# An encoder layer on one NeuronCore: order of the vector work behind a head norm, order of the indexer's items, other PSUM banks for the sample's products, a later spill and a later residual scaling

## The chip, the core and the metric

The kernel runs on one NeuronCore of one Trainium2 chip, in one launch. The metric is the time on the device in microseconds, and lower is better. The kernel before takes 1190.45 us, the median of three runs (1190.23 to 1190.97).

## What is computed

One layer of a streaming encoder, in float32, for two groups of tokens that share all weights: 512 tokens of a prompt and 32 tokens of a sample. They are handled as one block of 544 columns, two halves of 272. The model width is 1024.

```python
x = post_norm(x, swiglu1(modulate(x, sh1, sc1)), 1 + gt1, 0.5)
h = modulate(x, sh2, sc2)
rq, rk, rv, rg, aq, ak, av, iq, ik, iw = split(h @ w_in)      # 33 blocks of 128 columns
ret = head_norm(retention(rq, rk, rv)) * silu(rg)             # 4 heads, chunkwise recurrence
score = sum_over_heads(iw * relu(iq @ ik.T))                  # the indexer, 8 heads
keys  = top_k(score, 128)                                     # admissible keys alone
att   = softmax(aq @ ak[keys].T) @ av[keys]                   # 8 heads; rotary on aq, ak, iq, ik
x = post_norm(x, concat(ret, att) @ w_out, 1 + gt2, 1.0)
x = post_norm(x, swiglu2(modulate(x, sh3, sc3)), 1 + gt3, 0.5)
```

`post_norm` is a layer norm of `ALPHA * x + weight * gate * out`. The sample also has 512 earlier keys and values and an earlier retention state, which are inputs. Outputs are the new x of both groups, their keys, values and indexer keys, and the retention states.

## The kernel before

**Products.** Each operand of a large product is split into a high and a low part (`float32r`); a product is three matmuls (`mm3`, line 140). A weight block of 128 columns is loaded raw (`wr_w`, on SP's queue), ScalarE rounds it (line 129, a CAST) and negates the rounded part (line 133), and a DMA on GpSimd's queue adds the raw block to that, which leaves the low part (line 134). For some blocks VectorE subtracts instead (line 136). A weight is split three products ahead of its use (`AHEAD`, `next_w`).

**Order of the work.** The order of TensorE's instructions is written by hand: each matmul is tied to the one before (`ordered("pe", ...)`, lines 66 to 78; the tie is an order of issue, not a wait). The raw loads are tied in the same way. The other engines' orders are made by the framework when the program is built: where an engine is free in its own model of the times, it takes among the instructions that are ready the one that was written first. On the chip each engine then runs its list in that fixed order, and an instruction whose input is late holds up all behind it. `tc.high_priority()` puts the instructions written inside it ahead of others that are ready; `add_manual_dep(..., NOSYNC)` only fixes that one comes behind another in such a list.

**Ticks.** Side work is written as Python generators (`jobs`, lines 81 to 98). The main line calls `tick()` after each half of a projection, which is 24 matmuls of 272 columns; a job that says `yield n` goes on n ticks later. So a tick is a place in the written order, about 3 to 5 us of TensorE's time in the middle stage.

**The middle stage** (the mixer), about 440 to 720 us. The main line projects `h` on 33 weight blocks: indexer first, then for each retention head hh its q, k and v (`retention`, line 853), then for each pair c of attention heads its k, q and v (`pair_inputs`, line 975), then four gates (line 1159). Beside it run these jobs:

- `indexer` (line 752): ten items. An item is 6 to 12 products of indexer queries `iq[c]` with the keys `iks`, for a token tile t of 128 rows and c's of two heads each; into two PSUM banks (one of tag `l`, one of tag `o`), which ScalarE's relu empties (line 767) and VectorE adds up into `work[t]` (lines 772, 774). Tile 1 takes two items, tiles 2 and 3 four each. Then the sample's two groups (`isg`, line 782) follow.
- `topk` (line 796), for tiles 1, 2, 3 and the sample: 16 or 17 steps of MAX8 (line 803) and MATCH_REPLACE8 (line 804) each on VectorE, two steps a tick for the tiles, one for the sample. It begins when tile 1 has its scores, and sets the flag `("mask", t)` when a tile is done.
- `side` of each retention head (line 879): its products, then `head_norm` (line 939), a chain of small VectorE operations on the products that ScalarE copied (line 917); two ticks later ScalarE applies it (line 925, five operations), and one tick later TensorE transposes the result (`rot`, line 929).
- `roped` of each pair (line 986): rows of k and q that take part in the rotary go by DMA to `rp`, VectorE turns them (`rope_turn`, lines 624 to 626), they go back, and `parts` (lines 646, 647) splits k and q.
- `attention` (line 1062): for each pair three groups n of tiles: `logits` (`lg`, two banks of tag `l`), a tick or two later the transposes of the weights (`pt`, two banks of tag `t`), then the products with the values.
- `sample_attention(g)` (line 1013), g = 0 and 1: waits for `("mask", 's')` and for a pair's attention; its logits go into two banks (`sl`, `sl2`), two ticks later transposes into two more (`spt`, `spt2`), which ScalarE copies (lines 1044, 1046).
- `spill` (line 816): x, in the four tiles `xr`, goes to DRAM to make room; `reload` (line 1131) brings it back, and scales it by the layer norm in eight steps, one a tick: two VectorE operations (line 1138) and one on ScalarE (line 1140). The output projection adds to it (line 270).

**PSUM** has eight banks: three of tag `a` (which the projections' halves use in turn), two of `l`, two of `t`, one of `o`. A product into a bank waits until the bank's last reader is done.

Of the kernel before, what the change touches and what calls it, by code (L numbers as in the profile page):

```python
# [16 lines left out]
P = 128  # L17
# [20 lines left out]
def encoder_layer_kernel(ctx, tc, xT, cT, wc1, w_e, w_cond, b_condT, lnp, w_gu1, w_dn1, w_in, w_out, w_gu2, w_dn2,  # L38
# [51 lines left out]
    def spawn(job):  # L90
        resume(job, now[0] + 1)
# [31 lines left out]
    def split_w(raw, n, name, lo_eng=None, pool=None, pin=False, src=None):  # L123
        if pool is None:
            hl = wh.tile([P, 2, ND, P], FR, name=f"wh_{name}", tag="wh")
            hi, lo = hl[:, 0], hl[:, 1]
        else:
            hi, lo = (pool.tile([P, ND, P], FR, name=f"wu_{name}", tag="u") for _ in range(2))
        c = nc.scalar.copy(hi[:, :n, :], raw[:, :n, :])  # L129
        if pin:  # L130
            tc.keep_in_program_order(c)
        if src is not None and lo_eng is None:
            nc.scalar.mul(lo[:, :n, :], hi[:, :n, :].bitcast(F32), -1.0)  # L133
            nc.gpsimd.dma_start(lo[:, :n, :], src, accum_op=ALU.add)  # L134
        else:
            r = (lo_eng or nc.gpsimd).tensor_tensor(lo[:, :n, :], raw[:, :n, :], hi[:, :n, :].bitcast(F32), op=ALU.subtract)
            last["lo"] = r.ins.name
        return hi, lo
# [482 lines left out]

    def rope_turn(rp, *zs):
        r = rp[0:32 * len(zs)]
        behind(nc.vector.stream_shuffle(r[:, 1, :], r[:, 0, :], SWAP), "evac")
        nc.vector.tensor_mul(r, r, tabA[0:32 * len(zs)])
        nc.vector.tensor_add(r[:, 0, :], r[:, 0, :], r[:, 1, :])
        for slot, z in enumerate(zs):
            nc.sync.dma_start(z[ROT], rp[32 * slot:32 * slot + 32, 0, :])
# [123 lines left out]
    def indexer():  # L752
        nc.vector.memset(work[0], 0.0)
        nc.vector.memset(work[0][0:64, 64:128], NEG)
        flags.add(("mask", 0))
        yield 0
        for t in range(1, 4):
            L = P * (t + 1)
            acc = work[t]
            n = 512 // L  # L760
            for c in range(0, 4, n):
                pair = [bank("l", "isc"), bank("o", "isc")]
                pair_products([[p[:, L * e:L * e + L] for e in range(n)] for p in pair],
                              [(iq[c + e], iks, t) for e in range(n)])
                for s in range(2):
                    rl = scr("rl")
                    nc.scalar.activation(rl[:, :n * L], pair[s][:, :n * L], AF.Relu)
                    for e in range(n):
                        hh = 2 * (c + e) + s
                        r, f = rl[:, L * e:L * e + L], iw[:, t, hh:hh + 1]  # L770
                        if hh == 0:
                            nc.vector.tensor_scalar(acc, r, f, None, op0=ALU.mult)
                        else:
                            nc.vector.scalar_tensor_tensor(acc, r, f, acc, op0=ALU.mult, op1=ALU.add)
                yield 1
            nc.vector.memset(acc[0:64, L - 64:L], NEG)
            flags.add(("score", t))
            if t == 1:
                spawn(topk())
        psA, psB = bank("a", "iss"), bank("o", "iss2")  # L780
        for g in range(2):
            ps, p2 = bank("l", "isg"), bank("l", "isg2")
            lq = iqz[:, 128 * g:128 * g + 128]
            mm(ps, lq, cik, start=True, stop=True)
            mm(p2[:, 0:32], lq, ikn, start=True, stop=True)
            rl = scr("rls")
            nc.vector.tensor_scalar(rl[:, 0:512], ps, 0.0, iws[:, g:g + 1], op0=ALU.max, op1=ALU.mult)
            nc.vector.tensor_scalar(rl[:, 512:544], p2[:, 0:32], 0.0, iws[:, g:g + 1], op0=ALU.max, op1=ALU.mult)
            yield 1
            mm(psA, sel, rl[:, 0:512], start=(g == 0), stop=(g == 1))  # L790
            mm(psB[:, 0:32], sel, rl[:, 512:544], start=(g == 0), stop=(g == 1))
        nc.scalar.copy(work['s'][:, 0:512], psA)
        nc.scalar.copy(work['s'][:, 512:544], psB[:, 0:32])
        flags.add(("score", 's'))

    def topk():
        for t, rate in ((1, 2), (2, 2), (3, 2), ('s', 1)):
            while ("score", t) not in flags:
                yield 1
            w = work[t]  # L800
            for n in range(17 if t == 's' else 16):
                m8 = sm.tile([P, 8], F32, name="m8", tag="m8")
                behind(nc.vector.max(m8, w), "pe")  # L803
                nc.vector.match_replace(w, in_to_replace=m8, in_values=w, imm_value=MARK)  # L804
                if n % rate == rate - 1:
                    yield 1
            nc.vector.tensor_scalar(w, w, -3.3e38, NEG, op0=ALU.is_gt, op1=ALU.mult)
            if t != 's':
                L = P * (t + 1)
                nc.vector.memset(w[0:64, L - 64:L], NEG)  # L810
            flags.add(("mask", t))
# [2 lines left out]
    project(taken(qs[3]))  # L814

    def spill():
        yield 0
        for j in range(4):
            nc.sync.dma_start(xd[j], xr[j].rearrange("p a t -> p (a t)"))

# [32 lines left out]
    def retention(hh):  # L853
# [25 lines left out]
        def side():  # L879
# [39 lines left out]
            nc.vector.scalar_tensor_tensor(so2, S0, GAM[hh] ** 32, ps2, op0=ALU.mult, op1=ALU.add)  # L919
            nc.sync.dma_start(st_s[hh], so2)  # L920
            normed = [(on[:, n * P:(n + 1) * P], P) for n in range(4)] + [(on2[0:32], 32)]
            w = head_norm(normed)
            yield 2
            for j, (x, rows) in enumerate(normed):
                nc.scalar.activation(x, x, AF.Identity, bias=w[:rows, 2, j:j + 1], scale=w[:rows, 1, j:j + 1])
# [13 lines left out]
    def head_norm(parts):  # L939
# [12 lines left out]
        for _ in range(3):  # L952
            nc.vector.scalar_tensor_tensor(z, y, -0.5, y, op0=ALU.mult, op1=ALU.mult)
            nc.vector.tensor_tensor(z, z, v, op=ALU.mult)
            nc.vector.scalar_tensor_tensor(y, z, 1.5, y, op0=ALU.add, op1=ALU.mult)
        nc.vector.scalar_tensor_tensor(w[:, 2], mv[:, :, 0], -1.0, w[:, 1], op0=ALU.mult, op1=ALU.mult)
        return w


# [53 lines left out]
    def sample_attention(g):  # L1013
# [5 lines left out]
        if g == 0:  # L1019
            yield 3  # L1020
        yield from wait_for(("mask", 's'), ("att", 2 * g + 1))
        ps, p2 = bank("l", "sl"), bank("l", "sl2")
        for j in range(4):
            c = 2 * g + j // 2
            lq = Vs[c][:, 1, 32 * (j % 2):32 * (j % 2) + 32]
# [10 lines left out]
        nc.vector.tensor_max(m, mx[:, 0:1], mx[:, 1:2])  # L1036
        softmax_rows(Pt, m)
        yield 2
        pt, pt2 = bank("t", "spt"), bank("t", "spt2")
        for t in range(4):  # L1040
            turned(pt[:, t * P:(t + 1) * P], Pt[:, t * P:(t + 1) * P], ident)
        turned(pt2[0:32, 0:P], Pt[:, 512:544], ident)
        PT = pu[:, 1, 0:512]
        nc.scalar.copy(PT, pt)
        PT2 = half_scr("PsT2", [P, P])
        nc.scalar.copy(PT2[0:32], pt2[0:32, 0:P])
        yield 1
        po = bank("l", "spo")
        pcs = [po[own(j % 2), 32 * (j // 2):32 * (j // 2) + 32] for j in range(4)]
# [81 lines left out]
    def reload():  # L1131
        for j in range(4):
            load(xr[j].rearrange("p a t -> p (a t)"), xd[j])
        yield 3
        for d in range(ND):
            x = xv(xr, d)
            for i, (a, b) in enumerate(HALVES):
                behind(nc.vector.scalar_tensor_tensor(x[:, a:b], x[:, a:b], al1[0][:, d:d + 1], rs1[i], op0=ALU.mult,
                                                      op1=ALU.mult), "pe")
            nc.scalar.activation(x, x, AF.Identity, bias=al1[1][:, d:d + 1])  # L1140
            yield 1
# [197 lines left out]
```

## Time and profile before

| | us |
|---|---|
| median of the runs | 1190.45 |
| the profiled execution: its own time | 1189.48 |
| its span, first to last instruction | 1187.4 |
| TensorE busy in it | 1159.3 |
| VectorE, ScalarE, GpSimd busy | 665.8, 586.7, 199.7 |

The profile is of one execution. "PE" is TensorE's matmuls, "PEld" its weight loads, "DVE" VectorE, "ACT" ScalarE, "POOL" GpSimd, "SP" the queue that issues most DMAs. L75 is line 75, the helper through which all matmuls go, L78 that of the transposes, so that groups are told apart by the names of tiles: `isc<-iks,iqs` is a product into the tile `isc`. In the timeline a row is: start, duration, engine, line, operation, output<-inputs, shape, how many; in brackets the idle time before it and what ended that. In the windows' table each row is one stretch of time, with the busy time of each engine, the clock that TensorE was granted (1.00 is full), the busy share of the DMA engines and GB/s.

### The profile page before, as it was taken

To read this page: it belongs to the slowest core of one execution; us is meant where nothing else is said; L and a number is where in the kernel's file an instruction comes from. 1 tells how busy PE (TensorE), PEld (TensorE's weight loads), DVE (VectorE), ACT (ScalarE), POOL (GpSimd) and SP (SyncE) were. 2 spreads that over 40 slices of the span, in tenths; PEclk is the share of its full clock that TensorE was granted. 3 is DMA by queue.
4 is the path that set the end of the run, shared out by engine and by line. 5 is a ranking of instruction groups with operands and counts; after the bars stand their busy time and mean duration, and the time that the engine had idled before them with its cause. 6 is when DMAs were issued, how large, how long until landed. Compare 5 with 4: busy or idle time off the path is not lost.

```text
span 1187.4 us, 23002 instructions
## 1 busy us (share of the span) xinstructions
PE 1159.3 (98%) x9419; PEld 1127.8 (95%) x9419; DVE 665.8 (56%) x1574; ACT 586.7 (49%) x990; POOL 199.7 (17%) x231
## 2 busy tenths in 40 slices
PE   9999999999999999899989999999999999999995
PEld 7999999999999999789979989999999999999995
DVE  5767665764468484677887775885542222201416
ACT  3644444444335364655466577546444444433423
POOL 0112111111111303312111101104111111111110
PEclk9999999999999999999989999999999999999998
DMA  9899999997999466644845588807988878788842
GB/s 359 293 297 308 239 256 229 258 215 183 296 259 215 119 222 168 149 116 115 193 100 162 132 257 225 209 31 197 263 177 175 177 175 173 163 173 176 177 88 76
DMA packets 71451, 231.41 MB, mean 195 GB/s; under 512 B 8657, under 2 KB 12881, under 8 KB 71345
## 3 DMA queue, kind: packets, MB, share of 16 engines
q0 software_dynamic: 23472, 83.37, 40.3%
q1 hardware_dynamic: 47728, 146.43, 35.5%
q8 instruction: 74, 1.21, 0.4%
q14 instruction: 33, 0.26, 0.1%
q10 hardware_dynamic: 144, 0.14, 0.0%
HBM read 220.54 MB, written 7.35 MB: 192 GB/s over the span
## 4 chain that ended last, share of the span: by engine, by line
PE 89%; DVE 4%; DMA 4%; ACT 2%; issue 1%; SPq 0%; DVEq 0%; ACTq 0%
PE gu L75 40%; PE dn L75 26%; PE in L75 15%; DMA we_raw<-in_w_e 3%; PE gu_e L75 2%; PE po L75 1%; PE pt L78 1%; DMA wh_w<-in_w_gu 1%; PE ro L75 1%; PE lg L75 1%; PE isc L75 1%; ACT wh_w L129 0%; DMA cm<-in_cmat 0%; DVE wk L804 0%; ACT wh_w L133 0%
## 5 line engine op out<-in xcount | busy, mean ns | idle before, releaser
L75 PE MATMUL gu<-h,wh_w 128*128 128x272 f32 x3840 | 482.7, 288 | 0.6 <-DMA wh_w<-in_w_gu 0.6
L75 PEld LDWEIGHTS gu<-h,wh_w 128*128 128x128 f32 x3840 | 481.4, 188 | 0.8 <-DMA wh_w<-in_w_gu 0.8
L75 PE MATMUL dn<-hid,wh_w 128*128 128x272 f32 x2112 | 266.6, 288 | 0.0
L75 PEld LDWEIGHTS dn<-hid,wh_w 128*128 128x128 f32 x2112 | 265.4, 188 | 0.2
L129 ACT CAST wh_w<-wr_w 128x1024 fp32r<-128x1024 f32 (+1 forms) x162 | 165.6, 1024 | 152.9 <-PE dn L75 102.1
L75 PE MATMUL in<-h,wh_w 128*128 128x272 f32 x1392 | 189.9, 294 | 0.0
L75 PEld LDWEIGHTS in<-h,wh_w 128*128 128x128 f32 x1392 | 179.6, 191 | 5.3 <-issue 3.4
L133 ACT ACTIVATE wh_w<-wh_w 128x1024 fp32r<-128x1024 f32 (+1 forms) x158 | 163.7, 1037 | 2.9
L556 DVE SCALAR_TENSOR_TENSOR ca<-wc,cz,ca 128x1024 f32<-128x1024 f32 x98 | 129.7, 1349 | 26.5 <-DMA wc<-in_w_cond 26.2
L134 POOL DMA_DIRECT2D wh_w<-in_w_gu x79 | 69.2, 876 | 408.8 <-ACT wh_w L133 333.6
L190 DVE TENSOR_TENSOR tnh<-tnh,gu 128x272 f32<-128x272 f32 x80 | 35.0, 437 | 123.1 <-PE gu L75 123.1
L188 ACT ACTIVATE tnh<-gu 128x272 f32<-128x272 f32 x80 | 31.8, 397 | 112.9 <-PE gu L75 112.7
L189 DVE SCALAR_TENSOR_TENSOR tnh<-tnh,gu 128x272 f32<-128x272 f32 x80 | 34.7, 435 | 84.3 <-ACT tnh L188 84.1
L191 ACT CAST hid<-tnh 128x272 fp32r<-128x272 f32 x88 | 36.7, 418 | 88.9 <-DVE tnh L190 88.9
L134 POOL DMA_DIRECT2D wh_w<-in_w_dn x48 | 41.7, 870 | 224.7 <-ACT wh_w L133 215.4
L270 DVE SCALAR_TENSOR_TENSOR xq<-dn,C,xq 128x272 f32<-128x272 f32 (+2 forms) x48 | 18.0, 404 | 105.2 <-PE dn L75 105.2
L192 DVE TENSOR_TENSOR hid<-tnh,hid 128x272 fp32r<-128x272 f32 x88 | 40.7, 464 | 39.2 <-ACT hid L191 38.2
L134 POOL DMA_DIRECT2D wh_w<-in_w_in x29 | 25.3, 885 | 136.2 <-ACT Pu L964 30.9
L803 DVE MAX8 m<-wk 128x8 f32<-128x544 f32 (+3 forms) x65 | 38.8, 598 | 0.7
L804 DVE MATCH_REPLACE8 wk<-m,wk 128x544 f32<-128x544 f32 (+3 forms) x65 | 38.0, 584 | 0.0
L75 PE MATMUL gu_e<-h,we 128*128 128x272 f32 x192 | 27.3, 296 | 0.5 <-ACT h L510 0.4
L75 PEld LDWEIGHTS gu_e<-h,we 128*128 128x128 f32 x192 | 24.8, 188 | 2.4 <-issue 1.0
(266 smaller groups left out, 1103.1 us busy)
## 6 DMA issues: line engine op xcount, KB each, us to landing
wr_w<-in_w_gu SPq DMA_DIRECT2D x84, 512.0 KB, 5.5
wh_w<-in_w_gu POOLq DMA_DIRECT2D x79, 512.0 KB, 7.3
wc<-in_w_cond SPq DMA_DIRECT2D x56, 512.0 KB, 6.9
wr_w<-in_w_in SPq DMA_DIRECT2D x33, 512.0 KB, 5.3
wh_w<-in_w_in POOLq DMA_DIRECT2D x29, 512.0 KB, 6.8
wr_w<-in_w_dn SPq DMA_DIRECT2D x32, 448.0 KB, 4.0
wh_w<-in_w_dn POOLq DMA_DIRECT2D x32, 448.0 KB, 5.4
wc<-in_wc SPq DMA_DIRECT2D x16, 512.0 KB, 8.0
```

Of the source, the lines that this page charges most:

```text
L75: ordered("pe", nc.tensor.matmul(*a, **kw))
L129: c = nc.scalar.copy(hi[:, :n, :], raw[:, :n, :])
L133: nc.scalar.mul(lo[:, :n, :], hi[:, :n, :].bitcast(F32), -1.0)
L134: nc.gpsimd.dma_start(lo[:, :n, :], src, accum_op=ALU.add)
L188: nc.scalar.activation(t, pg, AF.Tanh, scale=0.5)
L189: nc.vector.scalar_tensor_tensor(t, t, 1.0, pg, op0=ALU.add, op1=ALU.mult)
L190: nc.vector.tensor_tensor(t, t, pu, op=ALU.mult)
L191: nc.scalar.copy(hid[:, 0, a:b], t)
L192: nc.vector.tensor_tensor(hid[:, 1, a:b], t, hid[:, 0, a:b].bitcast(F32), op=ALU.subtract)
L556: nc.vector.scalar_tensor_tensor(acc[r], w, c, acc[r], op0=ALU.mult, op1=ALU.add)
L803: behind(nc.vector.max(m8, w), "pe")
L804: nc.vector.match_replace(w, in_to_replace=m8, in_values=w, imm_value=MARK)
```

## The change

- `head_norm` is written inside `tc.high_priority()`, and the MAX8 of top-k and the shuffle of the rotary each come behind the last instruction of the latest head norm in VectorE's list.
- The indexer's ten items are taken in the order (1,0) (2,0) (1,2) (2,1) (2,2) (2,3) (3,0) to (3,3), t before c, where it was all of tile 1, of tile 2, of tile 3. The next weight's CAST that is written after the first item comes behind that item's second relu in ScalarE's list.
- `isg2` and `sl2` take a bank of tag `t` instead of `l`; `sl` and `spt` take one of `a` instead of `l` and `t`.
- The two copies behind `spt` are written inside `tc.high_priority()`, the small one first.
- The spill job begins three ticks later, the scaling in `reload` two ticks later.

```diff
--- before.py
+++ after.py
@@ -127,6 +127,8 @@
         else:
             hi, lo = (pool.tile([P, ND, P], FR, name=f"wu_{name}", tag="u") for _ in range(2))
         c = nc.scalar.copy(hi[:, :n, :], raw[:, :n, :])
+        if "relu" in last:
+            tc.add_manual_dep(c.ins, last.pop("relu"), NOSYNC, reason="order of issue")
         if pin:
             tc.keep_in_program_order(c)
         if src is not None and lo_eng is None:
@@ -621,7 +623,7 @@
 
     def rope_turn(rp, *zs):
         r = rp[0:32 * len(zs)]
-        behind(nc.vector.stream_shuffle(r[:, 1, :], r[:, 0, :], SWAP), "evac")
+        behind(behind(nc.vector.stream_shuffle(r[:, 1, :], r[:, 0, :], SWAP), "evac"), "norm")
         nc.vector.tensor_mul(r, r, tabA[0:32 * len(zs)])
         nc.vector.tensor_add(r[:, 0, :], r[:, 0, :], r[:, 1, :])
         for slot, z in enumerate(zs):
@@ -754,32 +756,34 @@
         nc.vector.memset(work[0][0:64, 64:128], NEG)
         flags.add(("mask", 0))
         yield 0
-        for t in range(1, 4):
+        for t, c in ((1, 0), (2, 0), (1, 2), (2, 1), (2, 2), (2, 3), (3, 0), (3, 1), (3, 2), (3, 3)):
             L = P * (t + 1)
             acc = work[t]
             n = 512 // L
-            for c in range(0, 4, n):
-                pair = [bank("l", "isc"), bank("o", "isc")]
-                pair_products([[p[:, L * e:L * e + L] for e in range(n)] for p in pair],
-                              [(iq[c + e], iks, t) for e in range(n)])
-                for s in range(2):
-                    rl = scr("rl")
-                    nc.scalar.activation(rl[:, :n * L], pair[s][:, :n * L], AF.Relu)
-                    for e in range(n):
-                        hh = 2 * (c + e) + s
-                        r, f = rl[:, L * e:L * e + L], iw[:, t, hh:hh + 1]
-                        if hh == 0:
-                            nc.vector.tensor_scalar(acc, r, f, None, op0=ALU.mult)
-                        else:
-                            nc.vector.scalar_tensor_tensor(acc, r, f, acc, op0=ALU.mult, op1=ALU.add)
-                yield 1
-            nc.vector.memset(acc[0:64, L - 64:L], NEG)
-            flags.add(("score", t))
-            if t == 1:
-                spawn(topk())
+            pair = [bank("l", "isc"), bank("o", "isc")]
+            pair_products([[p[:, L * e:L * e + L] for e in range(n)] for p in pair],
+                          [(iq[c + e], iks, t) for e in range(n)])
+            for s in range(2):
+                rl = scr("rl")
+                r = nc.scalar.activation(rl[:, :n * L], pair[s][:, :n * L], AF.Relu)
+                if (t, c) == (1, 0):
+                    last["relu"] = r.ins.name
+                for e in range(n):
+                    hh = 2 * (c + e) + s
+                    r, f = rl[:, L * e:L * e + L], iw[:, t, hh:hh + 1]
+                    if hh == 0:
+                        nc.vector.tensor_scalar(acc, r, f, None, op0=ALU.mult)
+                    else:
+                        nc.vector.scalar_tensor_tensor(acc, r, f, acc, op0=ALU.mult, op1=ALU.add)
+            yield 1
+            if c + n == 4:
+                nc.vector.memset(acc[0:64, L - 64:L], NEG)
+                flags.add(("score", t))
+                if t == 1:
+                    spawn(topk())
         psA, psB = bank("a", "iss"), bank("o", "iss2")
         for g in range(2):
-            ps, p2 = bank("l", "isg"), bank("l", "isg2")
+            ps, p2 = bank("l", "isg"), bank("t", "isg2")
             lq = iqz[:, 128 * g:128 * g + 128]
             mm(ps, lq, cik, start=True, stop=True)
             mm(p2[:, 0:32], lq, ikn, start=True, stop=True)
@@ -800,7 +804,7 @@
             w = work[t]
             for n in range(17 if t == 's' else 16):
                 m8 = sm.tile([P, 8], F32, name="m8", tag="m8")
-                behind(nc.vector.max(m8, w), "pe")
+                behind(behind(nc.vector.max(m8, w), "pe"), "norm")
                 nc.vector.match_replace(w, in_to_replace=m8, in_values=w, imm_value=MARK)
                 if n % rate == rate - 1:
                     yield 1
@@ -814,7 +818,7 @@
     project(taken(qs[3]))
 
     def spill():
-        yield 0
+        yield 3
         for j in range(4):
             nc.sync.dma_start(xd[j], xr[j].rearrange("p a t -> p (a t)"))
 
@@ -919,7 +923,8 @@
             nc.vector.scalar_tensor_tensor(so2, S0, GAM[hh] ** 32, ps2, op0=ALU.mult, op1=ALU.add)
             nc.sync.dma_start(st_s[hh], so2)
             normed = [(on[:, n * P:(n + 1) * P], P) for n in range(4)] + [(on2[0:32], 32)]
-            w = head_norm(normed)
+            with tc.high_priority():
+                w = head_norm(normed)
             yield 2
             for j, (x, rows) in enumerate(normed):
                 nc.scalar.activation(x, x, AF.Identity, bias=w[:rows, 2, j:j + 1], scale=w[:rows, 1, j:j + 1])
@@ -953,7 +958,8 @@
             nc.vector.scalar_tensor_tensor(z, y, -0.5, y, op0=ALU.mult, op1=ALU.mult)
             nc.vector.tensor_tensor(z, z, v, op=ALU.mult)
             nc.vector.scalar_tensor_tensor(y, z, 1.5, y, op0=ALU.add, op1=ALU.mult)
-        nc.vector.scalar_tensor_tensor(w[:, 2], mv[:, :, 0], -1.0, w[:, 1], op0=ALU.mult, op1=ALU.mult)
+        r = nc.vector.scalar_tensor_tensor(w[:, 2], mv[:, :, 0], -1.0, w[:, 1], op0=ALU.mult, op1=ALU.mult)
+        last["norm"] = r.ins.name
         return w
 
 
@@ -1019,7 +1025,7 @@
         if g == 0:
             yield 3
         yield from wait_for(("mask", 's'), ("att", 2 * g + 1))
-        ps, p2 = bank("l", "sl"), bank("l", "sl2")
+        ps, p2 = bank("a", "sl"), bank("t", "sl2")
         for j in range(4):
             c = 2 * g + j // 2
             lq = Vs[c][:, 1, 32 * (j % 2):32 * (j % 2) + 32]
@@ -1036,14 +1042,15 @@
         nc.vector.tensor_max(m, mx[:, 0:1], mx[:, 1:2])
         softmax_rows(Pt, m)
         yield 2
-        pt, pt2 = bank("t", "spt"), bank("t", "spt2")
+        pt, pt2 = bank("a", "spt"), bank("t", "spt2")
         for t in range(4):
             turned(pt[:, t * P:(t + 1) * P], Pt[:, t * P:(t + 1) * P], ident)
         turned(pt2[0:32, 0:P], Pt[:, 512:544], ident)
         PT = pu[:, 1, 0:512]
-        nc.scalar.copy(PT, pt)
         PT2 = half_scr("PsT2", [P, P])
-        nc.scalar.copy(PT2[0:32], pt2[0:32, 0:P])
+        with tc.high_priority():
+            nc.scalar.copy(PT2[0:32], pt2[0:32, 0:P])
+            nc.scalar.copy(PT, pt)
         yield 1
         po = bank("l", "spo")
         pcs = [po[own(j % 2), 32 * (j // 2):32 * (j // 2) + 32] for j in range(4)]
@@ -1131,7 +1138,7 @@
     def reload():
         for j in range(4):
             load(xr[j].rearrange("p a t -> p (a t)"), xd[j])
-        yield 3
+        yield 5
         for d in range(ND):
             x = xv(xr, d)
             for i, (a, b) in enumerate(HALVES):
```

## The prediction

> **What bounds the kernel now.** I read the page first, then the waits of TensorE, then the middle stage in the windows and the timeline.
>
> ```profile
> span 1187.4 us, 23002 instructions
> ...
> PE 1159.3 (98%) x9419; PEld 1127.8 (95%) x9419; DVE 665.8 (56%) x1574; ACT 586.7 (49%) x990; POOL 199.7 (17%) x231
> ...
> PE 89%; DVE 4%; DMA 4%; ACT 2%; issue 1%; SPq 0%; DVEq 0%; ACTq 0%
> ```
>
> TensorE is busy for 98% of the span and carries 89% of the chain that ended last. The change neither adds nor removes a matmul, so it can only gain what TensorE loses by waiting, and by a lower clock after a wait. The waits of TensorE (total, times, longest) that lie in the middle stage:
>
> ```profile
> PE rot L78 <- ACT rsB L925: 3.5, 1, 3.5
> PE isc L75 <- ACT rl L767: 2.6, 1, 2.6
> PE isg L75 <- DVE Dm L903: 1.6, 1, 1.6
> ...
> PE lg L75 <- DVE mx L970: 1.0, 1, 1.0
> PE isc L75 <- ACT iqs L646: 0.8, 1, 0.8
> PE pt L78 <- ACT Psu L1044: 0.7, 1, 0.7
> ...
> PE pt L78 <- ACT PsT L1046: 0.2, 1, 0.2
> PE isc L75 <- DVE iqs L647: 0.2, 1, 0.2
> ```
>
> Together 10.6 us. Two of these places have a low clock (in the windows the last three numbers are the granted clock, the DMA share and GB/s; ahead of them the busy times of PE, PEld, DVE, ACT, POOL):
>
> ```profile
> 469.56:473.66 4.10, 4.10 (x38) 3.82 (x37) 4.03 (x6) 2.36 (x3) 3.96 (x4) 1.00 0.88 334
> 473.66:479.17 5.51, 1.88 (x14) 1.08 (x13) 3.22 (x6) 5.51 (x9) 4.36 (x6) 0.98 0.46 86
> 479.17:483.70 4.53, 4.53 (x27) 4.53 (x25) 2.05 (x5) 1.16 (x3) 0.86 (x1) 0.64 1.04 269
> 587.34:604.37 17.03, 13.53 (x88) 12.41 (x89) 16.79 (x54) 7.61 (x16) 2.45 (x6) 0.83 0.70 168
> 596.40:606.50 10.10, 6.60 (x31) 5.60 (x31) 7.72 (x22) 4.20 (x10) 1.54 (x5) 0.66 0.58 133
> ```
>
> 0.64 stands right behind the indexer's waits, 0.66 holds the wait of `rot` and what follows.
>
> **Head norm: the wait of `rot` (3.5 us).** TensorE around it, and the same five transposes of an earlier head:
>
> ```profile
> 548.42 0.77 PE L78 MATMUL rot<-cm,rsB 128*128 128x128 f32 x5
> 549.12 0.25 PE L75 MATMUL rz<-rqk 128*32 128x32 f32 x2
> ...
> 587.23 9.28 PE L75 MATMUL in<-h,wh_w 128*128 128x272 f32 x72
> 600.00 1.87 PE L78 MATMUL rot<-cm,rsB 128*128 128x128 f32 x5 [3.50 <-ACT rsB L925]
> ...
> 606.47 0.60 PE L78 MATMUL vt<-cm,vz 128*128 128x128 f32 x4
> ```
>
> At the rate of the first 72 matmuls, 24 take 3.09 us, so from 587.23 to the `vt` it would be 4 x 3.09 + 0.70 (548.42 to 549.12) = 13.1 us. It was 19.2. The stall costs 6.1 us: 3.5 of wait and 2.6 of low clock. On VectorE:
>
> ```profile
> 588.21 0.48 DVE L946 BATCH_NORM_STATS2 bst<-rsB 128x6 f32<-128x128 f32 x2
> 588.60 0.17 DVE L947 BATCH_NORM_AGGREGATE bmv<-bst 128x2 f32<-128x6 f32 x1
> ...
> 599.28 0.14 DVE L956 SCALAR_TENSOR_TENSOR hnw<-bmv,hnw 128x5 f32<-128x5 f32 x1
> ```
>
> ```profile
> 505.78 0.17 DVE L953 SCALAR_TENSOR_TENSOR hnw<-hnw 128x5 f32<-128x5 f32 x1
> 505.98 0.16 DVE L954 TENSOR_TENSOR hnw<-hnw 128x5 f32<-128x5 f32 x1
> ```
>
> The norm takes 11.1 us there, because each of its small operations stands between two of top-k or the rotary. In the first head, where two stand together, they are 0.20 us apart. The twelve of them make 2.4 us, and the five pairs of 0.24 and 0.17 before them at most 2.1. With the edit the last ends near 588.2 + 4.5 = 592.7. Line 925 is five operations of ScalarE:
>
> ```profile
> 599.46 2.03 ACT L925 ACTIVATE rsB<-rsB,hnw 128x128 f32<-128x128 f32 x5 [1.58 <-DVE hnw L956]
> ```
>
> With their 2.0 us `rot` has its input near 594.7, ahead of 596.5, where the 72 matmuls end. So the whole 6.1 us goes if the lists come out as written.
>
> What is late next is what was pushed back: rotary and top-k, behind which `parts` and so `lg` of the first pair queue. TensorE comes 6.1 us sooner to that `lg`, and VectorE was busy for 16.79 of the 17.03 us from 587.34 to 604.37. Its slack is this:
>
> ```profile
> 607.21 0.28 DVE L837 COPY aV<-vts 32x128 f32<-32x128 f32 x1 [2.85 <-PE vts L78]
> ```
>
> If all that VectorE did before had to be done before `lg` and its softmax, only these 2.85 us could be kept, and 3.3 would come back as new waits. But the new item order starts top-k one tick later (below), so of the work before this place one tick's share, two steps, falls behind it. By the means of all 65 steps (the second number behind the bar, in ns) two steps are 2.4 us:
>
> ```profile
> L803 DVE MAX8 m<-wk 128x8 f32<-128x544 f32 (+3 forms) x65 | 38.8, 598 | 0.7
> L804 DVE MATCH_REPLACE8 wk<-m,wk 128x544 f32<-128x544 f32 (+3 forms) x65 | 38.0, 584 | 0.0
> ```
>
> The bounds are 0 and 3.3; I take 0.5, near the lower, as the two splits of `parts` are what `lg` really needs. The other three heads' `rot` do not wait (the row counts one wait).
>
> **Items of the indexer (3.6 us of waits).**
>
> ```profile
> 469.56 0.98 PE L75 MATMUL isc<-iks,iqs 64*128 64x256 f32 x12
> ...
> 473.66 0.39 PE L75 MATMUL isc<-iks,iqs 64*128 64x256 f32 x1
> ...
> 483.70 1.05 PE L75 MATMUL rs<-rqk 128*128 128x128 f32 x8
> ```
>
> An item and the half behind it took 4.1 us the first time (469.56 to 473.66) and 10.0 the second (to 483.70): 5.9 lost, 3.6 in waits and 2.3 in low clock. The second item waits first for relu (2.6: the bank of tag `o` is single), then for the split of the last queries (0.8 + 0.2). Item (2,0) in its place needs only the first queries, so the latter 1.0 goes. The relu wait does not, as far as the trace shows. ScalarE:
>
> ```profile
> 471.27 1.05 ACT L129 CAST wh_w<-wr_w 128x1024 fp32r<-128x1024 f32 x1 [2.03 <-DMA wr_w<-in_w_in]
> ...
> 475.49 1.07 ACT L767 ACTIVATE rl<-isc 128x512 f32<-128x512 f32 x2
> ```
>
> Two CASTs with their second steps stand ahead of relu and were written ahead of it (weights are split three products early); the first of them waits for its load. The new tie holds only the next CAST, written later and already behind relu here. The low clock may stay or go with one wait of 2.6 where there were three: the row with 0.64 follows three, the one with 0.66 a single wait of 3.5, and nothing stands between. So of its 2.3 I count half: 1.0 + 1.2 = 2.2 us, between 1.0 and 3.3. [...] `topk` starts a tick later, and with it all four masks. The masks of the tiles are still set a tick before the `lg` that asks for each; the sample's is set one tick later, and as `sl` waits for it, `sl` and all behind it move one tick. The sample's products are wanted only in the second half of the output projection, several ticks later.
>
> **Banks (1.6 + 1.0 + 0.9 us).** `isg2` waited for VectorE to empty an `l` bank; the two `t` banks were emptied ticks before, so 1.6 goes. `lg` waited 1.0 for the banks of `sl`; it no longer shares them. `sl2` now needs a `t` bank, which in the old tick would have just been filled by `vt`; one tick later it is free. `pt` waited 0.7 + 0.2 for the banks of `spt`; `spt` is now in `a`, and one tick later than that `pt`. Only `spt2` still shares `t`, and its copy goes first. Three `a` banks serve one half each in turn, and one more tenant leaves a half two ticks to be emptied. Nothing new is late here unless ScalarE's list is unlucky; bounds 0 and 3.5 for all three, I take 3.5.
>
> **Spill and scaling: nothing.**
>
> ```profile
> 432.28 3.55 SPq L819 DMA_DIRECT2D x_spill<-xr  x4
> ...
> 467.64 1.38 SPq L72 DMA_DIRECT2D wr_w<-in_w_in  x3
> ```
>
> The spills were written four ticks ahead of the indexer's first item (469.56), which at some 3.2 us a tick is near 457, yet SP issued them at 432: the written place does not hold them, only x being free. Three ticks later should not hold them either, so I count 0. The scaling is held, by its tie to TensorE:
>
> ```profile
> L1138 DVE SCALAR_TENSOR_TENSOR xq<-xq,ag,lny x16: 484/494/497, 699.0 to 733.2; 128x272 f32<-128x272 f32 x16
> L270 DVE SCALAR_TENSOR_TENSOR xq<-dn,C,xq x14: 243/496/503, 724.4 to 758.1; 128x272 f32<-128x272 f32 x8, 128x240 f32<-128x240 f32 x3, 128x32 f32<-128x32 f32 x3
> ```
>
> Two ticks (some 8 us) later its last step ends near 741, and the addition of that block comes as the eighth, seven halves of some 3.1 us after 724.4, at 746. If that cover of 5 us went, the second-last bank would wait, below 3 us. I take 0.
>
> **The sum** for the profiled execution: 6.1 + 2.2 + 3.5 - 0.5 = 11.3 us, 1189.48 to 1178.2. The runs' median, 1190.45, is 0.97 above that execution, so 1179.2 for it.
>
> **Rivals.** All below from 1190.45.
> - *VectorE becomes the bound.* Behind the norm, top-k and rotary are late for a TensorE that comes sooner; 3.3 instead of 0.5 comes back: 1182.0. For it: 16.79 of 17.03. Against: the share that moves a tick.
> - *The bank waits return at the next users* of `t` and `a` (a late copy on ScalarE): 3.5 lost, 1182.7.
> - *The spill does move, and helps.* Without its 2.23 MB the loads ahead land sooner, the CASTs are done before relu, and 2.6 + 1.1 more goes: 1175.5.
> - *The spill does move, and hurts: slower.* On SP it would stand ahead of the three loads of 467.64. Its issue takes 3.55 us; its 2.23 MB (four tiles of 128 rows of 1088 floats) need 6.7 us at the 334 GB/s of that window, and 12.0 at the mean of 430 to 480 us:
>
> ```profile
> DMA packets 3416, 9.31 MB, mean 186 GB/s; under 512 B 512, under 2 KB 1024, under 8 KB 3412
> ```
>
> The CAST of 471.27, and relu behind it in ScalarE's list, come 10.3 to 15.6 later, and `isc` waits for that. Against the 9.1 of the other edits and the 1.0 of the queries that is 0.2 to 5.5 slower, and 1.1 more with the clock: 1191 to 1197, say 1194. It decides from the point where that load lands 10 us later.
> - *The lists don't come out as written*: the ties bind order alone, and a norm that is still late, or a new wait elsewhere, takes the gain: 1188 to 1191.
>
> **How the numbers follow.** Forecast 0.50, VectorE 0.14, banks 0.08, spill helps 0.13, spill hurts 0.07, lists 0.08. A measurement here can tell about 0.2%, 2.4 us, from no change. Faster by over that: 0.50 + 0.14 + 0.08 + 0.13 = 0.85; same 0.08; slower 0.07. The range reaches from 1173.5 (spill helps, and all the clock) to 1187 (both middle rivals together, and a wait or two not seen), which leaves out the last two.
>
> **What would show it.** In the waits of TensorE: no `rot`, no `isg`, no `lg` <- L970, no `pt` <- L1044; `isc` <- L767 still 2.6. The twelve `hnw` operations 0.2 us apart. Spill at 432, its issue 35 us ahead of the three loads. `sl` one tick later, next to `lg` of 384 columns. The granted clock near 597 to 607 at 1.00. I am wrong if `rot` still waits over 1 us, if `lg` or `pt` near 600 to 615 waits instead, or if SP issues the spill among the loads of the first retention head.

## The result

After takes 1182.53 us, the median of four runs (1180.3 to 1185.22); before, run beside it, takes 1190.62 (1190.23 to 1190.97). The ratio is 0.9939, with a 95% interval from 0.9915 to 0.9963: 4.4 to 10.1 us faster. The forecast was 1179.2 in a range from 1173.5 to 1187.

The profiled execution of after takes 1182.54 us, with a span of 1180.5. Against the profiled execution of before both are 6.9 less, where the sum of the prediction was 11.3 less. Line numbers have moved: 767 is now 768, 646/647 are 648/649, 925 is 930, 956 is 961, 970 is 976, 624 to 626 are 626 to 628. The head of the page and the waits of TensorE:

```profile
span 1180.5 us, 23007 instructions
```

```profile
PE isc L75 <- ACT rl L768: 2.2, 1, 2.2
PE lg L75 <- ACT aqs L648: 1.3, 1, 1.3
...
PE lg L75 <- DVE mx L976: 1.2, 1, 1.2
```

`rot`, `isg` and both `pt` are gone from the list, as forecast, and so is `isc` for the queries. `isc` for relu is still there. New is `lg` for `aqs`: the first logits now wait for the split of the queries (and 0.3 more for its second part). `lg` for `mx` has the old name, but it is another wait, at another tile. TensorE's rows at the places that matter:

```profile
468.90 0.98 PE L75 MATMUL isc<-iks,iqs 64*128 64x256 f32 x12
...
472.99 0.44 PE L75 MATMUL isc<-iks,iqs 64*128 64x384 f32 x1
475.67 0.79 PE L75 MATMUL isc<-iks,iqs 64*128 64x384 f32 x5 [2.24 <-ACT rl L768]
476.39 4.82 PE L75 MATMUL in<-h,wh_w 128*128 128x272 f32 x24
481.05 1.05 PE L75 MATMUL rs<-rqk 128*128 128x128 f32 x8
...
524.53 3.25 PE L75 MATMUL in<-h,wh_w 128*128 128x272 f32 x24
...
591.97 0.77 PE L78 MATMUL rot<-cm,rsB 128*128 128x128 f32 x5
...
595.78 0.60 PE L78 MATMUL vt<-cm,vz 128*128 128x128 f32 x4
...
597.75 0.44 PE L75 MATMUL lg<-aks,aqs 64*128 64x128 f32 x4 [1.26 <-ACT aqs L648]
598.48 0.73 PE L75 MATMUL lg<-aks,aqs 64*128 64x128 f32 x8 [0.29 <-DVE aqs L649]
599.14 4.80 PE L75 MATMUL in<-h,wh_w 128*128 128x272 f32 x24
...
609.51 0.87 PE L78 MATMUL pt<-cm,Pu 128*128 128x128 f32 x6
...
691.59 1.49 PE L75 MATMUL lg<-aks,aqs 64*128 64x512 f32 x6 [1.16 <-DVE mx L976]
...
713.62 3.19 PE L75 MATMUL dn<-mx,wh_w 128*128 128x272 f32 x24
```

The same places of before that the prediction did not show:

```profile
528.91 3.25 PE L75 MATMUL in<-h,wh_w 128*128 128x272 f32 x24
...
616.01 0.88 PE L78 MATMUL pt<-cm,Pu 128*128 128x128 f32 x6
...
721.22 1.05 PE L75 MATMUL dn<-mx,wh_w 128*128 128x272 f32 x7
```

Subtracting each start from the one before it gives the account of the 6.9 us:

| stretch of TensorE's list | before | after | difference | forecast |
|---|---|---|---|---|
| start of the first `isc` | 469.56 | 468.90 | -0.7 | 0 |
| to `rs` (indexer's second item) | 483.70 | 481.05 | -2.0 | -2.2 |
| to the half behind `isg` | 528.91 | 524.53 | -1.7 | -1.6 |
| to `vt` (`rot` and its clock) | 606.47 | 595.78 | -6.3 | -6.1 |
| to the first `pt` | 616.01 | 609.51 | **+4.2** | +0.5 |
| to `dn` (sample, pairs) | 721.22 | 713.62 | -1.1 | -1.9 |
| to the end of the span | 1187.4 | 1180.5 | +0.7 | 0 |

Each term of the change came out within 0.2 us up to `vt`; the first 0.7 us lie ahead of the change and belong to no term. Right behind `vt` 4.2 us are given back: 1.55 of waits; 1.5 in a half of 24 matmuls that takes 4.80 instead of 3.29 at a low clock; 0.8 in the next two `lg`, at a clock of 1.00; and 0.3 in the first `lg`, which the waits break in pieces. In the windows (the third number from the right is the granted clock):

```profile
476.39:481.05 4.66, 4.66 (x25) 4.66 (x25) 2.45 (x5) 2.69 (x6) 1.64 (x3) 0.63 1.00 234
592.67:595.78 3.11, 3.11 (x26) 3.11 (x25) 2.97 (x7) 0.93 (x3) 0.47 (x2) 1.00 0.94 222
599.14:603.88 4.74, 4.74 (x27) 4.59 (x25) 4.74 (x23) 2.58 (x6) 0.87 (x1) 0.64 0.33 55
```

Behind `rot` the clock is 1.00, where before had 0.66. Behind relu's wait and behind the new wait it is 0.63 and 0.64.

The 0.8 us are short waits for VectorE, too short for the list of the waits: `lg` of 384 and of 512 columns take 1.08 and 1.35 us up to the next row, where before had 0.72 and 0.89. The weight loads of the second bank wait 0.18 and 0.28 us there until VectorE has masked what stood in it; at 512 columns:

```profile
608.62 0.53 PEld L75 LDWEIGHTS lg<-aks,aqs 64*128 64x128 f32 x5 [0.28 <-DVE mx L976]
```

**Why `lg` waits.** SP's queue and ScalarE:

```profile
590.58 0.34 SPq L72 DMA_DIRECT2D wr_w<-in_w_in  x1
591.59 1.15 SPq L630 DMA_DIRECT2D aqk<-rp  x2
```

```profile
595.46 0.62 ACT L648 CAST aks<-aqk 128x512 fp32r<-128x512 f32 x1 [2.18 <-DMA aqk<-rp]
597.08 0.62 ACT L648 CAST aqs<-aqk 128x512 fp32r<-128x512 f32 x1 [1.00 <-DMA aqk<-rp]
```

The rotary's return (`aqk<-rp`) is issued 1 us behind a weight load of 512 KB, and ScalarE starts on its two parts 3.9 and 5.5 us after the first issue. The ties behind the norm made the framework write SP's list in another order: with the norm's edits alone (below), this one load is the only difference between its list and that of before. The diff has no line that says so.

### The profile page after: what moved, and what is told of

Same layout as the page of the kernel before. It is cut to its first block, busy times and chain, and to the rows that moved or that the text cites. A ratio compares the mean times of both kernels' runs of the same rounds, so it can differ in the third digit from the quotient of the medians.

```text
span 1180.5 us, 23007 instructions
## 1 busy us (share of the span) xinstructions
PE 1157.6 (98%) x9419; PEld 1126.5 (95%) x9419; DVE 667.3 (57%) x1574; ACT 587.8 (50%) x990; POOL 200.3 (17%) x231
## 4 chain that ended last, share of the span: by engine, by line
PE 87%; DMA 5%; DVE 5%; ACT 2%; SPq 1%; issue 1%; DVEq 0%; ACTq 0%
PE gu L75 41%; PE dn L75 26%; PE in L75 12%; DMA we_raw<-in_w_e 3%; PE gu_e L75 2%; PE po L75 1%; PE pt L78 1%; PE lg L75 1%; DMA wr_w<-in_w_in 1%; PE isc L75 1%; ACT wh_w L129 1%; PE ro L75 1%; DMA ix<-ix 1%; ACT wh_w L135 0%; DVE ht L350 0%
```

## The experiments

Theory: the parts act separately, each as the prediction has it, and the new wait is for SP's order. Rivals: VectorE is the bound behind the norm; or the waits move from place to place as long as TensorE comes sooner. All runs are timed beside runs of before on the same chip (medians there 1191.65, 1190.17 and 1190.55 in the three groups), so ratios are compared.

**The norm's edits alone** (before, with these lines of the change, shortened here):

```diff
-        behind(nc.vector.stream_shuffle(...), "evac")
+        behind(behind(nc.vector.stream_shuffle(...), "evac"), "norm")
-                behind(nc.vector.max(m8, w), "pe")
+                behind(behind(nc.vector.max(m8, w), "pe"), "norm")
-            w = head_norm(normed)
+            with tc.high_priority(): w = head_norm(normed)
```

> Before with the head norm's edits alone (norm's operations first, top-k's MAX8 and the rotary's shuffle behind its end). First theory: the wait of rot and its low clock go (-6.1 us), and lg of the first pair then waits for the rotary's return, which SP now issues behind a load of 512 KB, 1.3 to 1.6 us of wait with some 1.5 us of low clock: about 3 us faster than before, 1187.5. Rival, the return stays in time: 6 us faster, 1184.5. Rival, VectorE is the bound: the new wait is named DVE rather than ACT and is 3 us or longer, 1187.8. In all three the wait of isg (1.6), of isc for relu (2.6), of lg for mx (1.0) and of pt (0.7) stay.

Measured: 1188.68 us, ratio 0.9980 (0.9964 to 0.9995), 2.4 us faster. The longest of TensorE's waits:

```profile
PE lg L75 <- ACT aqs L646: 1.7, 1, 1.7
```

`rot` is not in the list, `isg` waits 1.6 as before and `isc` for relu 1.4; and the wait for `aqs` is there without any other edit. The first theory holds: by the starts of the same rows, the stretch to `vt` (525.67 to 596.91) is 6.3 us shorter than in before, and the one to the first `pt` (to 610.67) 4.2 longer.

**The item order alone** (before, with the new loop over `(t, c)`).

> Before with the indexer's items in the other order alone. First theory: the waits of isc for iqs (0.8 and 0.2) go, the one for relu stays at 2.2 to 2.6 us, and the low clock behind it stays: 1 us faster, 1189.5. Rival, the low clock goes with a single wait: 2 to 3.3 us faster, 1187.3 to 1188.5, with a granted clock near 1.00 where before had 0.64. The wait of rot stays at about 3.5 in both.

Measured: 1191.68 us, ratio 1.0000 (0.9982 to 1.0019): nothing. Both expectations missed a wait, the longest of TensorE's here:

```profile
PE lg L75 <- DVE mx L972: 3.9, 1, 3.9
```

`rot` waits 3.5 and `isc` for relu 3.3; the wait for the queries is gone. But `sl` moves a tick later, as the prediction had it, and in this kernel it still holds both `l` banks: `lg` of 384 columns right behind it waits 3.9 us until VectorE has masked the sample's logits. In after, `sl` is in an `a` bank, and that `lg` has no wait. So without the other banks the item order gives back what it gains; no run has these two parts alone together.

**The banks alone** (before, with the four bank tags and the two copies of the change).

> Before with the other banks and the two copies alone. First theory: the waits of isg (1.6), lg for mx (1.0) and pt (0.7 and 0.2) go and nothing takes their place: 3.5 us faster, 1187.0. Rival, without the tick that the item order shifts, sl2 stands next to vt and waits for its bank: only 2 to 3 us faster, with a wait named sl of 0.3 us or more. Rival, the gain of lg needs the sample's mask a tick later or sooner: lg for mx still waits 1 us. The wait of rot stays at about 3.5.

Measured: 1188.69 us, ratio 0.9972 (0.9960 to 0.9985), 3.3 us faster. No `isg`, no `pt`; `lg` for `mx` is left with 0.8 in two waits, at the 512 columns. As forecast but for that remainder.

**The residual's spill undone** (`yield 3` back to `yield 0`). The program built from this has the same list of instructions on every engine as after, so the run also shows what one program does by itself.

> After with the residual's spill written at its old place. Theory: the written place of the spill binds nothing, so this is after over again: 0.994 of before with after's waits (lg for aqs 1.3, lg for mx 1.2, isc for rl 1 to 3), and its spread of times shows what one program does by itself. Rival, the later place helps or hurts by its traffic: over 2.4 us away from after and the load behind relu's CAST lands over 1 us elsewhere.

Measured: 1185.98 us (1183.02 to 1188.81), ratio 0.9963 (0.9948 to 0.9977). The median is 3.5 above after's, and in the profiled run the CAST before relu starts at 474.83 instead of 470.33. Both pass the marks set for the rival, though it is the same program: so the marks were too narrow, and the theory stands on the lists, not on this time. The intervals of the two ratios overlap from 4.4 to 6.2 us faster; that is the best that can be said of the size of the change.

**The scaling undone** (`yield 5` back to `yield 3` in `reload`).

> After with the residual's scaling at its old place, two ticks sooner. Theory, the scaling is off the path: after's time within 1.5 us and the same waits, 0.9945 of before. Rival, its place matters for VectorE at the sample's first softmax near 690 us: the wait of lg for mx (1.2) is 0.5 us longer or shorter or dn waits over 0.5 us, and the time moves by 1.5 us or more.

Measured: 1185.55 us, ratio 0.9966 (0.9952 to 0.9980), no different from the program above. But a wait appeared that neither theory named:

```profile
700.90 0.55 PE L78 MATMUL pt<-cm,Pu 128*128 128x128 f32 x3 [1.47 <-ACT PsT L1052]
```

```profile
699.37 1.04 ACT L129 CAST wh_w<-wr_w 128x1024 fp32r<-128x1024 f32 x1
700.32 0.39 ACT L1161 ACTIVATE rgt<-in 128x272 f32<-128x272 f32 x1
700.61 0.24 ACT L1052 COPY PsT<-spt 32x128 f32<-32x128 f32 x1
```

At the old place of the scaling, ScalarE's list has a CAST and the gate ahead of the second of the two copies behind `spt` (the first is at 698.91), and `pt` waits for the second. In after they stand together (697.35 and 697.84). The later scaling is thus worth a wait of 1.5 us, not nothing; end to end that is too little to tell.

**SP's order** (after, with a tie that puts the one weight load behind the rotary's return; shortened here):

```diff
+        if "back" in last and last["loads"] == 5:
+            behind(r, "back")        # r: the load's DMA; "back": the return's
```

> After with one of SP's loads (512 KB) put behind the rotary's return instead of ahead of it. Theory, the new wait of the first lg is for SP's order: the return lands 2 us after its issue instead of 3.9 to 5.5, the waits for aqs (1.3 and 0.3) go, and with them the low clock of the tick behind (1.5): about 3 us faster than after, 0.9915 of before. Rival, VectorE is what is late: the return is issued as late as in after, lg waits for it within 0.3 us of the 1.3, and the time is after's.

Measured: 1183.92 us, ratio 0.9951 (0.9933 to 0.9968). SP and TensorE:

```profile
593.24 1.15 SPq L630 DMA_DIRECT2D aqk<-rp  x2
594.47 0.53 SPq L72 DMA_DIRECT2D wr_w<-in_w_in  x1
```

```profile
598.75 0.73 PE L75 MATMUL lg<-aks,aqs 64*128 64x128 f32 x8 [0.24 <-DVE aqs L649]
...
604.70 0.44 PE L75 MATMUL lg<-aks,aqs 64*128 64x384 f32 x1 [2.02 <-DVE mx L976]
```

The return is first and the wait for `aqs` is gone (0.24 is left): SP's order was its cause, though the splits also moved by a place in the lists of VectorE and ScalarE. ScalarE starts on the two parts 2.0 and 3.5 us after the first issue. But the time can't be told from after's, as the next `lg` waits 2.02 for its two banks. VectorE, which must mask the logits before these banks are free:

```profile
600.85 0.28 DVE L976 CUSTOM_DVE_ANT_0 Pu<-lg,wk 128x128 f32<-128x128 f32 x1
...
601.72 0.28 DVE L976 CUSTOM_DVE_ANT_0 Pu<-lg,wk 128x128 f32<-128x128 f32 x1
...
604.24 0.40 DVE L976 CUSTOM_DVE_ANT_0 Pu<-lg,wk 128x256 f32<-128x256 f32 x1
```

Four maskings of 0.3 to 0.4 us, and the third starts 3.4 us after the first. Between them lie top-k's steps and the rest of the first softmax. In before, the last tile's mask was set at 604.26, ahead of the first `lg` at 607.11.

**The second item in another bank** (after; tag `t` instead of the single `o` for item (2,0)).

> After with one bank changed: the second item of the indexer takes its second half from t instead of from the single o. First theory, the wait for relu is for the bank: 2.2 us of wait and 1.6 us of low clock go, 3.8 us faster than after, about 1178.5. Rival, only the wait goes and the low clock comes elsewhere, or the third item waits instead, as relu itself is as late as before: 0 to 2 us faster than after, 1180.5 to 1182.5, with a wait of isc for rl of 1 us or more at a later item.

Measured: 1180.94 us, ratio 0.9914 (0.9896 to 0.9933). The rival's words fit better: the third item now waits 1.9 us for a relu (that of the second item, by the times), though its clock stays full (the half behind it takes 3.30), and TensorE, 2.2 us sooner at `vt`, waits 2.3 for `aqs` instead of 1.3. A bank hides a late relu for one item; it doesn't make it sooner. The time's interval overlaps after's.

**Both together.**

> After with both: the load behind the rotary's return, and the second indexer item in another bank. If the two waits are apart: the sum of the two, e_bank's 1.6 us under after and 3 us for the return, about 1178, 0.989 of before, with no wait of lg for aqs and isc for rl at the third item (1.9). Rival, TensorE comes sooner by what the bank gives and waits for the return all the same: a wait for aqs of 0.5 us or more, 1180.

Measured: 1181.36 us, ratio 0.9921 (0.9909 to 0.9934). No wait for `aqs`, but 2.04 at `lg` of 384 columns: 1178 was missed for the reason seen under SP's order.

**The maskings first** (both together, and VectorE's maskings ahead):

```diff
-                    masked(Pt, ps[:, a:b], work[t], mx)
+                    with tc.high_priority(): masked(Pt, ps[:, a:b], work[t], mx)
```

> best2 (load behind the rotary's return, second item's other bank) with the masking of lg put first on VectorE. Theory, the wait of 2.0 that came at lg of 384 columns is for the order on VectorE, four of top-k's operations (2.6 us) between the maskings: that wait and the 1.15 at lg of 512 columns for the sample's mask go, isc for rl (1.5) stays: 3 us faster than best2, 0.9895 of before. Rival, it is VectorE's amount of work: a wait of lg or pt for VectorE or for the exponentials of 1.5 us or more stands a tick later and the time is best2's.

Measured: 1177.90 us, ratio 0.9907 (0.9883 to 0.9930). TensorE runs through:

```profile
604.66 0.79 PE L75 MATMUL lg<-aks,aqs 64*128 64x384 f32 x6
605.38 3.27 PE L75 MATMUL in<-h,wh_w 128*128 128x272 f32 x24
```

The same work on VectorE in another order, and no wait of over 0.3 us follows there: it was the order, not the amount. (This profiled run, at 1185.6, is the longest of the six; it has waits of 2.7 and 1.2 for loads in the feed-forward parts.) The wait at the 512 columns did not go, it grew from 1.15 to 2.0. The ratio's interval overlaps that of the run before it, so the reading rests on the waits, not on the time.

**The sample's mask a tick sooner** (after; top-k's first step for the sample does not yield).

> After with top-k's first step for the sample a tick sooner, so that the sample's mask and with it sl stand where they stood in before. Theory, the wait of the 512-column lg for mx (1.2) comes from the sample's masking on VectorE right ahead of it: that wait goes, sl2 waits up to 0.4 us for the bank that vt has just filled: 0.8 to 1.5 us faster than after, 0.9930 of before. Rival, VectorE is late in any tick there: a wait for mx of 0.8 us or more stands at another lg, and the time is after's.

Measured: 1183.78 us, ratio 0.9951 (0.9939 to 0.9963). The 1.16 became two waits of 0.32 and 0.49 at the same place, and `sl` shows no wait: a third of it was for the tick. The time can't be told from after's.

**Two loads ahead of the indexer's returns** (after). Two of the weight loads that SP issued at 466 are written and tied so that they come behind the gathers and ahead of the four returns (shortened here):

```diff
+        early(g48)                   # two raw loads, behind the last gather
         rope_turn(rp, ikk, *qs[:3])  # its returns: behind these loads on SP
```

> After with two weight loads of 512 KB put ahead of the indexer's rotary returns on SP instead of behind them. Theory, relu of the first item is late because its CASTs wait for these loads, which SP issues only after four returns that wait for VectorE: both CASTs run before 470, the wait of isc for rl (1.4 to 3.7 in the runs so far) falls under 0.5 and the low clock behind it goes: 3.5 us faster than after, 0.9920 of before, and the times lie closer together. Rival, the loads' traffic delays the gather or the returns: the first isc or the queries' splits wait 1 us or more and the time is after's.

Measured: 1180.63 us, ratio 0.9926 (0.9904 to 0.9948). SP in after with its longest wait for these returns, then SP, ScalarE and TensorE here (lines behind 687 are 10 higher):

```profile
SPq L630 <- DVE rp L628: 5.3, 1, 5.3
```

```profile
461.42 2.55 SPq L630 DMA_DIRECT2D iqf<-rp  x3
...
466.42 1.38 SPq L72 DMA_DIRECT2D wr_w<-in_w_in  x3
```

```profile
453.84 3.90 SPq L697 DMA_DIRECT2D wr_w<-in_w_in  x2
460.08 0.53 SPq L630 DMA_DIRECT2D ix<-rp  x1
```

```profile
466.86 1.05 ACT L129 CAST wh_w<-wr_w 128x1024 fp32r<-128x1024 f32 x1
...
471.43 1.09 ACT L778 ACTIVATE rl<-isc 128x512 f32<-128x512 f32 x2
```

```profile
474.22 0.79 PE L75 MATMUL isc<-iks,iqs 64*128 64x384 f32 x6
```

Both CASTs are done before relu's input is there, `isc` waits for nothing, and the half behind it takes 3.29 instead of 4.82. The cause of relu's wait is shown: SP's queue was held up by returns that waited for VectorE, with loads behind them whose buffers were free (here they are issued at 454). In exchange a half ahead of the first `isc` waits 0.8 us for VectorE (`rqk`), and the first `isc` starts 1.2 us later than in after. The times did not lie closer together (1179.38 to 1187.65), so that part of the expectation failed.

**All four together.**

> All four together: two loads ahead of the indexer's returns, one behind the rotary's, the other bank, the maskings first. If the waits are apart: none of isc for rl, lg for aqs, lg for mx over 0.5 us is left, 7 us faster than after, about 1175.5, 0.9870 of before. Rival, TensorE coming sooner meets the next late thing each time: one wait of 1 us or more with its low clock stays, 1178.

Measured: 1178.14 us (1176.76 to 1179.34), ratio 0.9896 (0.9877 to 0.9915): 12 us faster than before, and faster than after, whose own interval begins where this one ends. The profiled run has a granted clock of 0.997 over the span, against 0.989 to 0.995 in the profiled runs of the other experiments. What is left:

```profile
PE lg L75 <- DVE mx L986: 1.5, 1, 1.5
```

`pt` waits 0.9 for the copy behind `spt`. The rival has the time (1178) and a wait of over 1 us that stays, but not its low clock: the halves behind the two waits take 3.24 and 3.25 us.

## Why the prediction was right or wrong

- **Head norm: right.** The twelve operations were to be 0.2 us apart. They are the first and the last of these, with ten between:

```profile
584.83 0.17 DVE L955 TENSOR_SCALAR hnw<-bmv 128x5 f32<-128x5 f32 x1
...
587.03 0.17 DVE L961 SCALAR_TENSOR_TENSOR hnw<-bmv,hnw 128x5 f32<-128x5 f32 x1
```

  `rot` comes without a wait, -6.3 for -6.1.
- **What is late next: wrong, and the step that failed.** "I take 0.5, near the lower, as the two splits of `parts` are what `lg` really needs": 4.2 came back, more than the upper bound of 3.3. That bound measured VectorE's slack. The splits were late for another reason, their input, which stood behind a load on SP (by the run with SP's order alone); and behind that stood the order of the maskings (by the run with the maskings first). The bound also left out that a wait can bring a low clock, 1.5 us of it on one half, and the short waits of the next two `lg` for VectorE, 0.8. The rival "VectorE becomes the bound" gave 1182.0, close to the time, but its mechanism did not decide: with the same work in another order the wait goes.
- **Indexer: right in size** (-2.0 for -2.2), in part by luck. The waits went from 3.6 to 2.2, 1.4 less for the 1.0 counted. Of the 1.2 counted for the clock nothing came: the half takes 4.66 instead of 4.53. In its place stands what the sum left out: the item of six products with one wait takes 0.7 us less than that of twelve with three (1.16 for 1.89 us, the waits taken off). The CASTs stand ahead of relu as the prediction read it, and the new tie does nothing: with the item order alone, which lacks the tie, ScalarE's list is the same around there. Of its bounds, 1.0 and 3.3, the lower applies to the clock's side: a single wait of 2.24 is followed by 0.63. And the wait is not one number: in the profiled runs of kernels that don't touch it, it is 1.4 (the norm alone), 2.3 (the banks alone), 2.5, 2.7, 3.6 and 3.7.
- **Banks: right for `isg` (-1.7) and `pt`; half right for `lg`.** The old wait of `lg` went; a wait of 1.16 took its place two groups on, as the sample's masking, one tick later, stands right ahead of that of `lg`. The tick was forecast; that `lg`'s banks wait behind that masking was not.
- **Spill: right.** The two programs have one list. **Scaling: right in the time, wrong in the reason**: it keeps ScalarE's two copies together, 1.5 us of wait at `pt`; the prediction named ScalarE's list as the danger of the banks, and did not tie it to this edit.
- The middle of the forecast was 3.3 too low by the median, and the profiled execution 4.3 above its sum; 3.7 of that is the 4.2 in place of 0.5.

## What to carry to other kernels

A tie between two instructions on one engine can change the lists of the others: read SP's list of the new program around each place that comes sooner, for small transfers that now stand behind a large one. When a wait is for a late copy, follow it to the first thing that was ready but not issued; here twice that was a load or a return on SP. Ask for the low clock behind a wait too: in after the half of 24 matmuls behind the waits of 1.26 and 0.29 us takes 4.80 us instead of 3.29, 1.5 us more, as much as many of the waits.

## What the runs showed of the hardware

In these runs the length of a wait does not tell whether the clock falls behind it. In the traces of before and after the granted clock is either 1.00 or 0.50. Between 30 and 1150 us it is 0.50 in two stretches of each: in before for 3.41 us from 478.97 and for 6.83 us from 598.44, in after for 3.41 us from 476.77 and from 599.65. The two starts lie 119.47 us apart in before and 122.88 in after, which is 35 and 36 times 3.413. Divided from these starts into slots of 3.413 us, the two traces have six slots at 1.00 in that time with TensorE busy for less than 2 us:

| run | slot | busy | the wait in it | clock of the next slot |
|---|---|---|---|---|
| before | 472.15 to 475.56 | 1.89 | `isc` for relu, its first part | 1.00 |
| before | 475.56 to 478.97 | 1.30 | `isc` for relu, its rest, and for the queries | 0.50 |
| before | 526.76 to 530.17 | 1.83 | `isg`, 1.57 us | 1.00 |
| before | 595.03 to 598.44 | 1.48 | `rot`, its first part | 0.50, and of the one after it |
| after | 473.36 to 476.77 | 1.17 | `isc` for relu, 2.24 us | 0.50 |
| after | 596.24 to 599.65 | 1.86 | `lg` for `aqs`, 1.26 and 0.29 us | 0.50 |

Here is a wait of 2.02 us in another run (SP's order alone, `lg` of 384 columns, 602.68 to 604.70; the half of 24 matmuls behind it takes 3.26 us):

```profile
600.79:604.20 3.41, 1.89 (x16) 1.66 (x14) 3.41 (x16) 1.26 (x5) 0.86 (x1) 1.00 0.55 79
604.20:607.61 3.41, 2.75 (x18) 2.25 (x19) 3.41 (x17) 1.21 (x4) 0.00 (x0) 1.00 0.47 93
```

And one of 2.04 us at the same `lg` (SP's order and the bank together, 598.09 to 600.13; the half behind it takes 5.57 us):

```profile
596.90:600.31 3.41, 1.37 (x11) 1.15 (x9) 3.41 (x18) 1.26 (x5) 0.24 (x1) 1.00 0.73 102
600.31:603.72 3.41, 3.37 (x13) 2.55 (x14) 3.41 (x14) 1.20 (x4) 0.00 (x0) 0.50 0.27 52
603.72:607.13 3.41, 3.41 (x16) 3.41 (x16) 2.24 (x9) 0.00 (x0) 0.00 (x0) 0.50 0.00 0
```

The first wait lies across two of the rows, TensorE is busy for 1.89 us of the one and 2.75 of the next, and the clock stays. The second lies in one row, with 1.37 us busy, and the next two rows are at half clock. In these rows and the table the clock falls behind 1.17, 1.30, 1.37, 1.48 and 1.86 us of busy time, and stays behind 1.83 and 1.89 (twice): no one number parts them. Why it falls, and why it stays low for a second 3.41 us in some cases, was not tested.

By an estimate from these lengths, half of 3.41 us, a low stretch in which TensorE is busy throughout costs up to 1.7 us, and one of 6.83 us up to 3.4. Measured at the halves behind the waits it is 1.5 us in after (4.80 for 3.29) and 2.3 with SP's order and the bank together (5.57 for 3.26, the half before the wait). Waits of nearly one length, 2.02 and 2.04 us, thus have a low clock behind them in one run and none in the other. That may be much of why one program's times spread: the six runs of the program that equals after lie 5.8 us apart, with clocks of 0.991 to 0.994; that is argued, not shown.
